# Two of the seven products of FFN layer two through an inner seven-product scheme

## The chip, the cores and the metric

The kernel runs on one core of a Trainium2 chip. A core has five engines with instruction streams of their own: TensorE (PE in the profile, with PEld for its weight loads), VectorE (DVE), ScalarE (ACT), GpSimd (POOL) and SyncE (SP), which here issues the DMA transfers. The engines wait for each other on semaphores. The metric is the device time of one launch in microseconds, lower is better; the kernel before stands at a median of 1946.75 us of three runs (1945.01 to 1947.24).

## The reference

One layer of a hybrid decoder block, for 2048 tokens of width 1024. The front half (a causal pooling mixer and a stick-breaking attention, each normalised, then an output projection) isn't touched. The change is in the feed-forward part behind it:

```python
h = h + jnp.einsum('bse,ed->bsd', mixed, w_out)
hn2 = rmsnorm(h, norm2_g)
up = jnp.einsum('bsd,df->bsf', hn2, w_up)      # 1024 -> 4096
act = jnp.square(jax.nn.relu(up))
h = h + jnp.einsum('bsf,fd->bsd', act, w_down) # 4096 -> 1024
return rmsnorm(h, final_g)
```

All of it is float32.

## The kernel before

A float32 product is made of three matmuls: each operand is split into a hi part (a copy as fp32r, on ACT) and a lo part (the difference, on DVE), and hi x hi, hi x lo and lo x hi are added up in PSUM. `split` does this, L143 on ACT and L144 on DVE.

Activations lie with features on the partitions; a tile is 128 features by T = 512 tokens. The 2048 tokens are four blocks of 512, taken as two pairs q = 0 and q = 1 (`PAIRS`). Both FFN layers multiply with a seven-product scheme (Strassen's, in Winograd's form): the pair gives the rows, features in and out are halved, and P1 to P7 take the place of eight quarter products. Layer one is the function `up`, layer two `down`.

`up` runs over 32 columns, 16 (number m) for each pair q, 7 products of 12 matmuls each (L1016). `post` makes the left operands of layer two from the products: A11, A12, A22 by relu and square on ACT (L949, L950), a21, and on DVE the sums S1 to S4 (L976, L979, L981, L989). `put` (L946) stores each to DRAM, in `sd[q][operand][chunk]`, from a ring of eleven tiles.

`down` goes through the products in the order P1 (A11), P6 (S2), P7 (S3), P4 (A22), P5 (S1), P3 (S4), each in 8 steps kk over both pairs, then P2 (A12) first for q = 0 and then for q = 1. A step loads one weight tile `wr` and a row tile `ar` for each pair (`make`, L1042 and L1073), splits them into `wd` and `ad`, and runs 48 matmuls (L1251; 2 pairs x 4 output chunks x 2 feature chunks x 3). Weight combinations are made on the way with `minus` (L1046) and two of them are kept in DRAM as `td` (L1048). PSUM's eight banks hold the 4 output chunks of both pairs; a sum that several products share goes on in its bank. After a product's last step `evac` copies a bank to SBUF (ACT, L1102) or adds it onto a value there (DVE, L1100). POOL adds the residual h (L1096), which SP loads into one of two `res` tiles (L1095). When both halves of an output block are done, `final` squares them (ACT, L1128) and sums the squares (DVE, L1129). The last two steps of P2 for q = 1 are held back and run in halves of 256 tokens, each with its end right behind it (`last_steps`, L1214).

`make` runs DA = 2 steps ahead in the code. The tile pools limit what can really be ahead: 3 row tiles (`rs`), 4 weight tiles (`rt`), 3 split weights (`t8`), 5 split rows (`s8`), 2 residual tiles (`rsp`). The pools of `down` are laid over memory that `up` has freed, and a tile waits for the last use of what lay there. A scheduler in the framework, with a model of times, sets the order of the instructions on each engine; the SP queue issues in that order, and an issue that has to wait holds all behind it.

The pools of `down` (name and number of tiles):

```python
rlp, tmp2, rs, rt, t8 = spool("rlp", 2), spool("tmp2", 2), spool("rs", 3), spool("rt", 4), spool("t8", DA + 1)
s8, pup, rsp = spool("s8", 2 * DA + 1), spool("pup", 8), spool("rsp", 2)
```

Of the kernel before, what the change touches and what calls it, by code (L numbers as in the profile page):

```python
# [8 lines left out]
F32 = mybir.dt.float32  # L9
# [37 lines left out]
def hymba_block(ctx: ExitStack, tc: tile.TileContext, xT, gains, w_in, pool_w, w_out, w_up, w_down, out):  # L47
# [88 lines left out]
    sd = [[[dram.tile([P, 2, T], F32, name=f"sd{q}_{i}_{c}") for c in range(8)] for i in range(7)] for q in range(2)]  # L136
    td = [[dram.tile([P, 2, T], F32, name=f"td{i}_{c}") for c in range(8)] for i in range(2)]
# [717 lines left out]
    def up(pools, more):  # L855
# [3 lines left out]
        cols = [(q, m) for q in range(2) for m in range(NM)]  # L859
# [14 lines left out]
        def load(q, m):  # L874
            raw[q, m] = (rbb if m % 2 else rba).tile([P, 4, G, P], F32, tag="rb", name="rb")
            nc.sync.dma_start(raw[q, m], w_up[m])
# [63 lines left out]
        def post(q, m, s):  # L940
# [4 lines left out]
            def put(i, t):  # L945
                nc.sync.dma_start(sd[q][i][m // 2][:, m % 2], t)  # L946
# [10 lines left out]
            if s == "P1":  # L957
                copy("p1")
            elif s == "P2":
# [32 lines left out]
        load(0, 0)  # L992
# [9 lines left out]
        load(0, 1)  # L1002
        lefts = [(g, q, s) for g, (q, m, s) in enumerate(slots) if m == 0 and not (q == 0 and s in order[:LB])]
        for g, (q, m, s) in enumerate(slots):
            while lefts and lefts[0][0] <= g + LA:
                make_left(*lefts.pop(0)[1:])
            if q == 0 and 4 <= m < 12 and m % 2 == 0 and s in SUMS:
                sums_second(m // 2 - 2, SUMS.index(s))
# [16 lines left out]
            if g + UA < len(slots):  # L1025
                make_weights(g + UA)
                q2, m2, s2 = slots[g + UA]
                n = q2 * NM + m2 + 2
# [3 lines left out]
    def down(pools):  # L1032
        t8, s8, rs, rt, pup, rsp, rlp, tmp_, psb = pools

        order = (("P1", A11), ("P6", S2), ("P7", S3), ("P4", A22), ("P5", S1), ("P3", S4), ("P2", A12))
        steps = [(n, i, kk, (0, 1)) for n, i in order[:-1] for kk in range(8)]
        steps += [("P2", A12, kk, (q,)) for q in range(2) for kk in range(8)]
        made = {}

# [10 lines left out]

        def make(g):
            n, i, kk, qs_ = steps[g]
            b11, b12, b21, b22 = range(4)
# [4 lines left out]
            elif n == "P6":  # L1058
                w = blk("t1", kk)
                minus(blk(b22, kk), w, 2, kk)  # L1060
# [3 lines left out]
            elif n == "P4":  # L1064
                w = blk("t2", kk)
                minus(blk(b21, kk), w)
            elif n == "P5":
                w = blk("t1", kk)
            else:
                w = blk(b22 if n == "P3" else b21, kk)  # L1070
# [9 lines left out]
            if extra is not None:  # L1080
                minus(blk(b12, kk), extra, 1, kk)
# [4 lines left out]
        CHAIN = {"P1": "p1", "P6": "u2", "P7": "u3", "P4": "c21"}  # L1086
# [11 lines left out]
        def evac(n_, q, n):  # L1098
            b, (j0, j1) = ps[q, n], PAIRS[q]
            add = lambda to, of: nc.vector.tensor_tensor(to[:, n], b, of[:, n], ALU.add)  # L1100
            if n_ in CHAIN:
                nc.scalar.activation(val(CHAIN[n_], q)[:, n], b, AF.Copy)  # L1102
                if n_ in ("P1", "P4"):
                    add_residual(val(CHAIN[n_], q)[:, n], j0 if n_ == "P1" else j1, 0, n)
            elif n_ == "P5":
                add(val("u3", q), val("u3", q))
                add_residual(val("u3", q)[:, n], j1, 1, n)
                add_residual(val("u2", q)[:, n], j0, 1, n)
                if n == 3:
                    final(j1, [val("c21", q)[:, k] for k in range(4)] + [val("u3", q)[:, k] for k in range(4)])  # L1110
            elif n_ == "P3":
                add(val("u2", q), val("u2", q))
                if q == 1:
                    last_half(n, val("u2", q)[:, n])
            else:
                add(val("p1", q), val("p1", q))
                if q == 0 and n == 3:
                    final(j0, [val("p1", q)[:, k] for k in range(4)] + [val("u2", q)[:, k] for k in range(4)])

# [40 lines left out]
        def last_half(n, c):  # L1160
            if n == 0:
                lastv["ss"] = tmp_.tile([P, T], F32, tag="ssl", name="ssl", bufs=1)
                lastv["c"] = {}
            squares(lastv["ss"], c, n == 0)
            lastv["c"][n] = c

        def last_turn():
# [3 lines left out]
            for n in range(4):  # L1171
                t = tmp_.tile([P, T], F32, tag="sq", name="fs")
                nc.scalar.activation(t, lastv["c"][n], AF.Copy, scale=gf[:, 4 + n:5 + n])
                for b in range(TB):
                    nc.tensor.transpose(half[b][:, n * P:(n + 1) * P], t[:, b * P:(b + 1) * P], ident)
            for b in range(TB):
                nc.scalar.activation(res[b // 2][:, b % 2, 1], half[b], AF.Copy)

        def last_steps(operands, j):

            dst = out[j].rearrange("k p t -> (k p t)").rearrange("(b t d) -> t b d", b=TB, d=D)
            ss, c11 = lastv["ss"], val("p1", 1)
# [10 lines left out]
            def finish(th, sq):  # L1193
# [6 lines left out]
                for i in range(2):  # L1200
                    b = 2 * th + i
                    o = lastv["res"][th][:, i]
                    nc.vector.tensor_scalar(o[:, 1], o[:, 1], y[:, i:i + 1], None, op0=ALU.mult)
                    nc.scalar.activation(o[:, 0], half[b], AF.Copy, scale=y[:, i:i + 1])
                    nc.sync.dma_start(dst[:, b], o)

            for th in range(2):
                cols = slice(th * W, (th + 1) * W)
                for n in range(4):
# [8 lines left out]
                    to = c11[:, n, cols]  # L1218
# [6 lines left out]
                    if n == 3:  # L1225
                        nc.vector.tensor_scalar(t, to, gf[:, n:n + 1], None, op0=ALU.mult)
# [202 lines left out]
```

## Time and profile before

| | |
|---|---|
| median of three runs | 1946.75 us (1945.01 to 1947.24) |
| span of the profiled execution, first to last instruction | 1941.4 us |
| the profiled execution's own time | the page gives its span alone |
| front, attention, output projection | 0 to 622 us |
| `up` | 622 to 1308.5 us, a column in 19.04 us |
| `down` | 1309 to 1941 us, a product in 87 us |
| DMA | 426.79 MB, mean 220 GB/s |

How to read it. The page gives the busy time of each engine as a share of the span, then the chain of work that ended last, followed back from the end. A group row reads: line, engine, operation, output tile<-input tiles, shape, count | total busy us, mean ns of one | idle us of the engine just ahead of it and what ended most of this idle time. A row of the timeline starts with start and length in us; `x12` is twelve instructions run together, and the bracket has the idle time ahead of it and its releaser. Rows with SPq are DMA issues. A row of the DMA view has the number of transfers, their size and the median us from issue to landing.

### The profile page before, as it was taken

How to read it: one execution, taken by the hardware profiler on the slowest of the kernel's cores; microseconds unless marked ns; L12 is line 12 of the kernel's file. 1: busy time of each engine (PE TensorE's matmuls, PEld its weight loads, DVE VectorE, ACT ScalarE, POOL GpSimd, SP SyncE). 2: the span in 40 equal slices, each digit the busy share in tenths (PEclk: the TensorE clock that was granted, in tenths of full speed). 3: DMA queues.
4: the chain of work that ended last, by engine and by line, in shares of the span. 5: the costliest groups of instructions: out<-in, count | busy, mean ns of one | idle time of the engine just before them, and what ended most of it. 6: DMA issues, size and time to landing. Idle time of an engine off the chain costs nothing.

```text
span 1941.4 us, 25998 instructions
## 1 busy us (share of the span) xinstructions
PE 1922.7 (99%) x9139; PEld 1605.2 (83%) x9139; DVE 1267.6 (65%) x1882; ACT 956.9 (49%) x1544; POOL 192.0 (10%) x399
## 2 busy tenths in 40 slices
PE   9999999999999999999999999999999999999997
PEld 7888888888888888888888888878888888888887
DVE  6887799668876975777586565665454443446474
ACT  5565566455544555555575555553323233424353
POOL 0211123102111110000000000000110000213010
PEclk9999999999999999999999999999999999999999
DMA  6685686888696954677564544477885554546472
GB/s 216 206 273 180 223 279 208 266 307 285 235 378 233 338 187 155 213 243 247 181 243 159 173 141 158 145 268 288 290 284 196 192 196 151 201 153 208 148 255 89
DMA packets 164845, 426.79 MB, mean 220 GB/s; under 512 B 19680, under 2 KB 25824, under 8 KB 160608
## 3 DMA queue, kind: packets, MB, share of 16 engines
q1 hardware_dynamic: 164560, 424.77, 64.1%
q8 instruction: 74, 1.21, 0.3%
q14 instruction: 67, 0.55, 0.1%
q10 hardware_dynamic: 144, 0.26, 0.0%
HBM read 284.44 MB, written 140.51 MB: 219 GB/s over the span
## 4 chain that ended last, share of the span: by engine, by line
PE 94%; DVE 3%; DMA 2%; ACT 1%; issue 0%; SPq 0%; DVEq 0%; ACTq 0%
PE pb L1251 31%; PE pY L1016 17%; PE pd L173 8%; PE pd L172 8%; PE pd L174 8%; PE pZ L1016 8%; PE pX L1016 4%; PE po L669 2%; PE pta L658 1%; PE pm L199 1%; PE pz L611 1%; PE pz L612 1%; PE pr L225 1%; DMA wr<-in_w_down_dram 1%; PE pb L1214 1%; PE pz L640 0%
## 5 line engine op out<-in xcount | busy, mean ns | idle before, releaser
L1251 PE MATMUL pb<-ad,wd 128*128 128x512 f32 x2640 | 601.6, 390 | 1.3 <-ACT ad L143 0.7
L1251 PEld LDWEIGHTS pb<-ad,wd 128*128 128x128 f32 x2640 | 494.8, 188 | 104.6 <-ACT ad L143 1.3
L1016 PE MATMUL pY<-sa,hw 128*128 128x512 f32 x1536 | 364.3, 390 | 1.2 <-ACT u L955 1.2
L1016 PEld LDWEIGHTS pY<-sa,hw 128*128 128x128 f32 x1536 | 288.1, 188 | 61.8 <-ACT u L955 2.1
L172 PE MATMUL pd<-h,hl 128*128 128x512 f32 x752 | 299.8, 399 | 0.7 <-DVE qkr L418 0.7
L173 PE MATMUL pd<-h,hl 128*128 128x512 f32 x752 | 297.2, 395 | 0.0
L174 PE MATMUL pd<-h,hl 128*128 128x512 f32 x752 | 297.0, 395 | 0.0
L143 ACT ACTIVATE ad<-ar 128x1024 fp32r<-128x1024 f32 x112 | 117.4, 1051 | 139.4 <-PE pb L1251 116.7
L1016 PE MATMUL pZ<-sa,hw 128*128 128x512 f32 x768 | 184.6, 389 | 0.0
L144 DVE TENSOR_TENSOR ad<-ar,ad 128x1024 fp32r<-128x1024 f32 x112 | 144.3, 1293 | 55.6 <-ACT ad L143 55.6
L144 DVE TENSOR_TENSOR wd<-wr,wd 128x1024 fp32r<-128x1024 f32 x64 | 82.2, 1285 | 148.9 <-ACT wd L143 148.4
L143 ACT ACTIVATE wd<-wr 128x1024 fp32r<-128x1024 f32 x64 | 67.8, 1059 | 206.0 <-PE pb L1251 198.3
L1016 PEld LDWEIGHTS pZ<-sa,hw 128*128 128x128 f32 x768 | 144.1, 188 | 29.8
L172 PEld LDWEIGHTS pd<-h,hl 128*128 128x128 f32 x752 | 142.2, 189 | 28.3 <-DVE qkr L418 1.0
L174 PEld LDWEIGHTS pd<-h,hl 128*128 128x128 f32 x752 | 141.9, 189 | 27.9
L173 PEld LDWEIGHTS pd<-h,hl 128*128 128x128 f32 x752 | 142.0, 189 | 26.8
L143 ACT ACTIVATE hl<-raw 128x512 fp32r<-128x512 f32 x168 | 104.2, 630 | 108.2 <-PE pd L174 69.9
L144 DVE TENSOR_TENSOR hl<-raw,hl 128x512 fp32r<-128x512 f32 x168 | 114.6, 687 | 51.3 <-ACT hl L143 50.9
L144 DVE TENSOR_TENSOR hw<-rt,hw 128x512 fp32r<-128x512 f32 x128 | 87.7, 688 | 76.3 <-ACT hw L143 76.1
L1016 PE MATMUL pX<-sa,hw 128*128 128x512 f32 x384 | 93.1, 389 | 0.0
L1046 DVE TENSOR_TENSOR wr<-wr 128x1024 f32<-128x1024 f32 x32 | 39.2, 1224 | 81.0 <-DMA wr<-in_w_down_dram 78.0
L955 ACT ACTIVATE u<-pY 128x512 f32<-128x512 f32 x64 | 38.1, 595 | 103.6 <-PE pY L1016 103.3
(203 smaller groups left out, 2389.7 us busy)
## 6 DMA issues: line engine op xcount, KB each, us to landing
ar<-sd SPq DMA_DIRECT2D x112, 512.0 KB, 4.5
wr<-in_w_down_dram SPq DMA_DIRECT2D x72, 512.0 KB, 3.7
rb<-in_w_up_dram SPq DMA_DIRECT2D x32, 1024.0 KB, 6.1
sd<-a SPq DMA_DIRECT2D x128, 256.0 KB, 3.7
raw<-in_w_in_dram SPq DMA_DIRECT2D x50, 512.0 KB, 4.4
sd<-s SPq DMA_DIRECT2D x96, 256.0 KB, 3.8
raw<-in_w_out_dram SPq DMA_DIRECT2D x32, 512.0 KB, 5.6
sr<-su SPq DMA_DIRECT2D x28, 512.0 KB, 5.5
```

The costliest lines, as they stand in the source:

```text
L143: nc.scalar.activation(hi, src, AF.Copy)
L144: return nc.vector.tensor_tensor(lo, src, hi.bitcast(F32), ALU.subtract)
L172: nc.tensor.matmul(ps, hl[:, 0, c], hi, start=(k == 0), stop=False)
L173: nc.tensor.matmul(ps, hl[:, 0, c], lo, start=False, stop=False)
L174: mm = nc.tensor.matmul(ps, hl[:, 1, c], hi, start=False, stop=(k == n - 1))
L199: marks["pm"] = nc.tensor.matmul(pm[:, c:c + 1], ss[:, c * P:(c + 1) * P], inv[n], start=(i == 0), stop=(i == len(parts) - 1))
L225: mm = nc.tensor.matmul(pr[:, b * P:(b + 1) * P], yr[:, x, b:b + 1].to_broadcast([P, P]), identr, start=(b == 0 and x == 0), stop=(b == TB ...
L669: nc.tensor.matmul(po[:, p * 256 + to:p * 256 + to + hi - lo], vw[:, 2 * p + v], at[:, x, lo:hi], start=(p == 0 and n == 0 and x == 0), sk ...
L955: nc.scalar.activation(k[name], y, AF.Copy)
L1016: nc.tensor.matmul(t, w[:, wx, c], a[:, ax, c % 2], start=first and c == 0 and x == 0, stop=last and c == G - 1 and x == 2, skip_group_che ...
L1046: nc.vector.tensor_tensor(b, a, b, ALU.subtract)
L1251: nc.tensor.matmul(ps[q, n], t[:, wx, c, n * P:(n + 1) * P], left_[q][:, ax, c], start=(n_ in ("P1", "P5", "P2") and kk == 0 and c == 0 an ...
```

## The change

P4 and P2 are no longer run as one product each with 8 steps. Each is a product of a 1024 x 2048 activation (512 tokens of either pair) and a 2048 x 512 weight quarter, and this is split again: the two token pairs give the two row blocks, the features in are halved (columns m and m + 8 of `up`), the 512 outputs are halved. Seven inner products of 4 steps with 12 matmuls take the place of 8 steps with 48. The order of the outer products is now P1, P6, P7, P4 (inner), P5, P2 (inner), and P3 last, for one pair after the other; so the tail works on c12 instead of c11.

What this brings with it:

- `up` takes its columns in the order m, m + 8 (`cols`), so that both halves of an inner row sum are near each other. In the second pair `inner_rows` loads the A22 and A12 tiles of the first pair back (`hr`, L871 of the new listing), and `inner_sums` makes four sums for each and stores them in `sdi` (L880 to L888); A22 and A12 of the first eight columns aren't stored for that pair.
- `inner_weights` makes the four inner weight differences and stores them in `wi`, for P4 during P7 and for P2 during P5 (`prepare`).
- `make_inner` loads and splits an inner step's operands: a weight tile (128 x 1024) holds two steps, a row tile one. `make_ahead` replaces the fixed lead: as many steps as 6 row tiles and 3 weight tiles allow.
- `inner_step` runs the 12 matmuls, and after an inner product's last step DVE adds the bank onto one quarter of the output (c21 or p1) in SBUF.
- P7's evacuation copies its bank twice (u3 and c21). P5's evacuation adds onto u3 and onto u2, the latter formerly in P3. So the squares of the finished blocks fall into P2.
- P6 makes and stores the second `td`, P4 did so before.
- `rs` has 5 tiles and `rt` 6.

```diff
-        cols = [(q, m) for q in range(2) for m in range(NM)]
+        cols = [(q, m + x * (NM // 2)) for q in range(2) for m in range(NM // 2) for x in range(2)]
...
+        def inner_rows(m):
+            for i in (A22, A12):
+                halves[i, 0] = r = srp.tile([P, 2, T], F32, tag="sr", name="hr")
+                for x in range(2):
+                    at = m + x * (NM // 2)
+                    nc.sync.dma_start(r[:, x], sd[0][i][at // 2][:, at % 2])
+
+        def inner_sums(m, i, t):
...
+            a, r = halves.pop((i, 1)), halves.pop((i, 0))
...
+            nc.vector.tensor_tensor(s1, a, t, ALU.add)
+            keep(0, s1)
+            nc.vector.tensor_tensor(s2, s1, r[:, 0], ALU.subtract)
+            keep(1, s2)
+            nc.vector.tensor_tensor(r[:, 0], r[:, 0], a, ALU.subtract)
+            keep(2, r[:, 0])
+            nc.vector.tensor_tensor(r[:, 1], r[:, 1], s2, ALU.subtract)
+            keep(3, r[:, 1])
...
-        order = (("P1", A11), ("P6", S2), ("P7", S3), ("P4", A22), ("P5", S1), ("P3", S4), ("P2", A12))
-        steps = [(n, i, kk, (0, 1)) for n, i in order[:-1] for kk in range(8)]
-        steps += [("P2", A12, kk, (q,)) for q in range(2) for kk in range(8)]
+        SPLIT = {"P4": A22, "P2": A12}
+        order = (("P1", A11), ("P6", S2), ("P7", S3), ("P4", A22), ("P5", S1), ("P2", A12))
+        steps = []
+        for n, i in order:
+            if n in SPLIT:
+                steps += [(n, p, kk, None) for p in ("P1", "P5", "P6", "P3", "P7", "P2", "P4") for kk in range(4)]
+            else:
+                steps += [(n, i, kk, (0, 1)) for kk in range(8)]
+        steps += [("P3", S4, kk, (q,)) for q in range(2) for kk in range(8)]
...
+        def make_inner(n, p, kk):
+            i, kp = SPLIT[n], kk // 2
+            if kk % 2 == 0:
+                if p in wi[i]:
+                    w = rt.tile([P, 4, 256], F32, tag="wr", name="wq")
+                    nc.sync.dma_start(w, wi[i][p][kp])
+                else:
+                    w = quarter(source[n], kp, *{"P1": (0, 0), "P2": (1, 0), "P3": (1, 1)}[p])
+                t = made["inner"] = t8.tile([P, 2, 4, 256], F32R, tag="wd", name="wd", align_bytes=256)
+            r = rs.tile([P, 2, T], F32, tag="ar", name="ar")
...
+            if kk % 2 == 0:
+                split((t[:, 0], t[:, 1]), w)
+            a = s8.tile([P, 2, 2, T], F32R, tag="ad", name="ad", align_bytes=256)
+            split((a[:, 0], a[:, 1]), r)
...
+                if n_ == "P7":
+                    nc.scalar.activation(val("c21", q)[:, n], b, AF.Copy)
+                    add_residual(val("c21", q)[:, n], j1, 0, n)
...
             elif n_ == "P5":
                 add(val("u3", q), val("u3", q))
                 add_residual(val("u3", q)[:, n], j1, 1, n)
+                add(val("u2", q), val("u2", q))
                 add_residual(val("u2", q)[:, n], j0, 1, n)
...
+        def inner_step(n_, p, kk, t, a):
+            tag, q, half = WHERE[p]
+            for i in range(2):
...
+                for c in range(2):
+                    for x, (wx, ax) in enumerate(((0, 0), (0, 1), (1, 0))):
+                        nc.tensor.matmul(b, t[:, wx, 2 * (kk % 2) + c, i * P:(i + 1) * P], a[:, ax, c],
...
+                if kk == 3:
+                    n, name = 2 * half + i, "c21" if n_ == "P4" else "p1"
+                    to = val(name, q)[:, n]
+                    nc.vector.tensor_tensor(to, b, to, ALU.add)
...
+            while ahead[0] < len(steps) and (ahead[1] + lefts(ahead[0]) <= 6 and ahead[2] + stationary(ahead[0]) <= 3):
...
-            rlp, tmp2, rs, rt, t8 = spool("rlp", 2), spool("tmp2", 2), spool("rs", 3), spool("rt", 4), spool("t8", DA + 1)
+            rlp, tmp2, rs, rt, t8 = spool("rlp", 2), spool("tmp2", 2), spool("rs", 5), spool("rt", 6), spool("t8", DA + 1)
```

How it moves the instructions, at the places that the prediction speaks of. The first is the SP queue at the seam of the two layers. A row has the line, the operation, what it writes<-reads, the shape, and in brackets the semaphores that it waits for (DMAHW0 to 7: transfers; the others: engines). Before, loads of `down` (L1042, L1073) stand among the stores of the last columns of `up` (`sd1_..._6` and `_7`, L946):

```order
L946 DMA sd1_5_6_415<-a21_12770 128x512 [waits DMAHW1_49,DVE_49]
L1073 DMA ar_13112<-sd0_0_0_313 128x1024 [waits DMAHW2_49,DVE_49]
L1073 DMA ar_13113<-sd1_0_0_369 128x1024 [waits DMAHW3_49]
L1073 DMA ar_13131<-sd0_0_1_314 128x1024 [waits DMAHW4_49]
L946 DMA sd1_1_6_383<-a12_12796 128x512 [waits DMAHW5_49,Activation_49]
L946 DMA sd1_6_6_423<-s4_12801 128x512 [waits DMAHW6_49,DVE_49]
L946 DMA sd1_0_7_376<-a11_12820 128x512 [waits DMAHW7_49,Activation_49]
L1042 DMA wr_13110<-in_w_down_dram 128x1024 [waits DMAHW0_49]
L1042 DMA wr_13125<-in_w_down_dram 128x1024 [waits DMAHW1_49,PE_49]
L1042 DMA wr_13129<-in_w_down_dram 128x1024 [waits DMAHW2_49]
L1042 DMA wr_13144<-in_w_down_dram 128x1024 [waits DMAHW3_49]
L946 DMA sd1_2_7_392<-a22_12875 128x512 [waits DMAHW4_49,Activation_49]
```

Now all loads of `down` (L1120, L1170) stand behind the last store, and the first waits for three transfers, two of them the stores from `hr_13121`:

```order
L977 DMA sd1_5_7_416<-a21_13267 128x512 [waits DMAHW5_49,DVE_49]
L977 DMA sd1_1_7_384<-a12_13290 128x512 [waits DMAHW6_49,Activation_49]
L880 DMA sdi1_0_3_428<-j1_13295 128x512 [waits DMAHW7_49,DVE_49]
L880 DMA sdi1_1_3_432<-j2_13296 128x512 [waits DMAHW0_49,DVE_49]
L977 DMA sd1_6_7_424<-s4_13305 128x512 [waits DMAHW1_49,DVE_49]
L880 DMA sdi1_2_3_436<-hr_13121 128x512 [waits DMAHW2_49,DVE_49]
L880 DMA sdi1_3_3_440<-hr_13121 128x512 [waits DMAHW3_49,DVE_49]
L1120 DMA wr_13350<-in_w_down_dram 128x1024 [waits DMAHW4_49,DMAHW3_49,DMAHW2_49]
L1170 DMA ar_13352<-sd0_0_0_313 128x1024 [waits DMAHW5_49]
L1170 DMA ar_13353<-sd1_0_0_369 128x1024 [waits DMAHW6_49]
L1120 DMA wr_13365<-in_w_down_dram 128x1024 [waits DMAHW7_49]
```

Moved: the loads of the first steps, from among the stores of the last two columns to behind all of them. On DVE at the same place, the inner sums of the last column pair (L882 to L888) are between the add that makes a12 (L1020) and the first split of `down` (L147):

```order
L1016 TENSOR_TENSOR a21_13267<-a11_13188,a21_13267 128x512 [waits DMAHW6_49]
L1020 TENSOR_TENSOR a12_13290<-pZ_13213,u2_13208 128x512 [waits DMAHW0_49,PE_49]
L882 TENSOR_TENSOR j1_13295<-a12_13165,a12_13290 128x512 [waits DMAHW2_49,Activation_49]
L884 TENSOR_TENSOR j2_13296<-j1_13295,hr_13121 128x512 [waits DVE_49]
L1024 TENSOR_TENSOR s4_13305<-a12_13290,s2_13273 128x512 [waits DMAHW6_49]
L886 TENSOR_TENSOR hr_13121<-hr_13121,a12_13165 128x512 [waits DVE_49]
L888 TENSOR_TENSOR hr_13121<-hr_13121,j2_13296 128x512
L147 TENSOR_TENSOR wd_13356<-wr_13350,wd_13356 128x1024 [waits DMAHW4_49,Activation_49]
L147 TENSOR_TENSOR ad_13359<-ar_13352,ad_13359 128x1024 [waits DMAHW5_49,Activation_49]
L147 TENSOR_TENSOR ad_13362<-ar_13353,ad_13362 128x1024 [waits DMAHW6_49,Activation_49]
```

Added there: j1, j2 and two `hr`; the splits of the first step, formerly between `up`'s last operations, are behind them. The third place is the SP queue where P5 ends, with the residual loads (`res`, L1095, now L1195) among the row loads of the next product. Before (the product is P3, `sd0_6`, `sd1_6`):

```order
L1073 DMA ar_15983<-sd1_6_2_419 128x1024 [waits DMAHW3_49,DVE_49]
L1095 DMA res_15851<-hs0_281 128x512 [waits DMAHW1_49,Pool_49]
L1095 DMA res_15861<-hs1_282 128x512 [waits Pool_49]
L1073 DMA ar_16045<-sd0_6_3_364 128x1024 [waits DMAHW5_49,DVE_49]
L1095 DMA res_15864<-hs0_281 128x512 [waits DMAHW4_49,DMAHW1_49,Pool_49]
L1095 DMA res_15874<-hs1_282 128x512 [waits DMAHW2_49,Pool_49]
L1095 DMA res_15877<-hs0_281 128x512 [waits DMAHW6_49,DMAHW4_49,Pool_49]
L1042 DMA wr_16232<-in_w_down_dram 128x1024 [waits DMAHW7_49,DVE_49]
L1095 DMA res_15911<-hs2_283 128x512 [waits DMAHW5_49,DMAHW0_49,Pool_49]
L1073 DMA ar_16046<-sd1_6_3_420 128x1024 [waits DVE_49]
```

Now (P2's inner products, rows from `sdi1`, `ar_16504` being the third row tile of inner product P6):

```order
L1195 DMA res_16257<-hs0_281 128x512 [waits DMAHW3_49,DMAHW1_49,Pool_49]
L1140 DMA ar_16463<-sdi1_1_0_429 128x1024 [waits DMAHW4_49,DVE_49]
L1195 DMA res_16267<-hs1_282 128x512 [waits DMAHW5_49,DMAHW2_49,Pool_49]
L1195 DMA res_16271<-hs0_281 128x512 [waits DMAHW6_49,DMAHW3_49,Pool_49]
L1195 DMA res_16305<-hs2_283 128x512 [waits DMAHW5_49,Pool_49]
L1195 DMA res_16309<-hs3_284 128x512 [waits DMAHW6_49,DMAHW0_49,Pool_49]
L1135 DMA wq_16624<-wi1_P7_0_461 128x1024 [waits DVE_49]
L1140 DMA ar_16470<-sdi1_1_1_430 128x1024 [waits DVE_49]
L1195 DMA res_16319<-hs2_283 128x512 [waits DMAHW7_49,Pool_49]
L1195 DMA res_16323<-hs3_284 128x512 [waits DMAHW4_49,DMAHW0_49,Pool_49]
L1140 DMA ar_16504<-sdi1_1_2_431 128x1024 [waits DVE_49]
```

Here a `res` load waits for POOL as before, but the row loads between them belong to steps of 12 matmuls instead of 48.

171 lines of the change are left out of this document (121 added, 50 removed).

## The prediction

> **What bounds the kernel now.** I read the page first: busy shares, chain, costliest groups.
>
> ```profile
> span 1941.4 us, 25998 instructions
> PE 1922.7 (99%) x9139; PEld 1605.2 (83%) x9139; DVE 1267.6 (65%) x1882; ACT 956.9 (49%) x1544; POOL 192.0 (10%) x399
> PE 94%; DVE 3%; DMA 2%; ACT 1%; issue 0%; SPq 0%; DVEq 0%; ACTq 0%
> L1251 PE MATMUL pb<-ad,wd 128*128 128x512 f32 x2640 | 601.6, 390 | 1.3 <-ACT ad L143 0.7
> ```
>
> TensorE is busy 99% and carries 94% of the chain that ended last. The second FFN layer (`down`, L1251) idles 1.3 us before 2640 matmuls. So a matmul taken out is worth its whole time, and a wait put in costs its whole time. The table by windows tells what the stages leave free (columns: length, PE, PE loads, DVE, ACT, POOL, clock, DMA share, GB/s): `up`, then P1, P7 and P5 with the start of P3 of `down`, then the tail.
>
> ```profile
> 1100.00:1200.00 100.00, 100.00 (x443) 82.83 (x442) 59.18 (x95) 53.44 (x94) 0.00 (x0) 1.00 0.42 147
> 1312.00:1400.00 88.00, 87.94 (x388) 72.83 (x389) 41.61 (x37) 31.14 (x35) 3.04 (x2) 1.00 0.79 280
> 1490.00:1580.00 90.00, 90.00 (x399) 74.53 (x398) 39.65 (x34) 29.95 (x33) 0.00 (x0) 1.00 0.60 195
> 1660.00:1760.00 100.00, 100.00 (x443) 82.82 (x442) 50.31 (x43) 34.56 (x39) 21.77 (x14) 1.00 0.53 175
> 1910.00:1941.00 31.00, 21.25 (x160) 20.06 (x158) 13.96 (x46) 11.51 (x25) 0.00 (x0) 0.91 0.29 111
> ```
>
> DVE is at 44 to 59%, ACT at 33 to 53%: room on average, so the places where order decides are looked at singly.
>
> **Removed: matmuls.** The chain gives the price of one: 12 in 2.72 us, 24 in 5.44.
>
> ```profile
> 1223.22 5.44 PE pY L1016 x24
> 1228.66 2.72 PE pX L1016 x12
> ```
>
> That is 0.2267 us each. P2 and P4 took 8 steps of 48, 384 each. An inner scheme takes 7 products x 4 steps x 12 = 336. 2 x 48 = 96 fewer: 96 x 0.2267 = **-21.8 us**. An inner product lasts 10.88 us, as one old step did.
>
> **Added at the seam of the two layers: a wait.** Before, the first loads of `down` are issued while `up` computes, and TensorE hardly pauses:
>
> ```profile
> 1278.90 1.27 SPq L1073 DMA_DIRECT2D ar<-sd  x3
> 1283.24 2.96 SPq L1042 DMA_DIRECT2D wr<-in_w_down_dram  x4
> 1305.64 2.88 PE L1016 MATMUL pZ<-sa,hw 128*128 128x512 f32 x12
> 1309.22 2.21 PE L1251 MATMUL pb<-ad,wd 128*128 128x512 f32 x8 [0.70 <-ACT ad L143]
> 1310.19 0.68 DVE L985 TENSOR_TENSOR a<-pZ,u 128x512 f32<-128x512 f32 x1
> 1311.61 0.63 ACT L950 ACTIVATE a<-a 128x512 f32<-128x512 f32 x1
> 1312.06 18.20 PE L1251 MATMUL pb<-ad,wd 128*128 128x512 f32 x79 [0.63 <-DVE ad L144]
> ```
>
> The last `up` matmul ends at 1308.52 (call it E). The pause is 0.70 + 0.63, and the 8 matmuls between took 2.21 instead of 1.81: 1.7 us in all. After the change the first `wr` tile lies over the last `hr` tile of the inner row sums, so its load waits for the last two stores from it, and on SP every first load of `down` stands behind that one. Nothing of `down` can then be prepared before `up` is wholly finished. The new chain, from rows of before: the add L985 starts at E+1.67, and the square of its result ends at 1312.24, E+3.72. Then five DVE operations (four inner sums and s4), 0.60 apart with 0.69 for the last:
>
> ```profile
> 1276.39 0.69 DVE L981 TENSOR_TENSOR a<-a,a 128x512 f32<-128x512 f32 x1
> 1276.99 0.69 DVE L985 TENSOR_TENSOR a<-pZ,u 128x512 f32<-128x512 f32 x1
> ```
>
> 3.1 us, to E+6.8. The store must land, then the load of `wr` and, on the same queue, of `ar`. Landing times, from `up` alone, over the whole page, and of `wr` around the seam, then the rate over 1255 to 1330 us in 40 slices:
>
> ```profile
> sd<-s SPq DMA_DIRECT2D x43, 256.0 KB, 2.2
> sd<-s SPq DMA_DIRECT2D x96, 256.0 KB, 3.8
> DMA to landing us min/median/max: 2.8/5.5/8.4
> GB/s 83 155 181 214 359 356 49 9 140 0 21 156 243 238 286 151 342 421 415 415 253 306 360 413 253 328 335 335 415 383 406 410 412 415 410 208 277 234 269 332
> ```
>
> With 2.2 for the store and 3.0 for a load with an empty queue: E+12.0. `ar`, 512 KB, comes 1.3 us behind it at the 415 GB/s that the busiest slices reach. The hi part of `wd`, meanwhile, and then that of `ad`, 1.05 us each on ACT:
>
> ```profile
> L143 ACT ACTIVATE ad<-ar 128x1024 fp32r<-128x1024 f32 x112 | 117.4, 1051 | 139.4 <-PE pb L1251 116.7
> L144 DVE TENSOR_TENSOR ad<-ar,ad 128x1024 fp32r<-128x1024 f32 x112 | 144.3, 1293 | 55.6 <-ACT ad L143 55.6
> ```
>
> First matmul at E+14.4, net of the old pause **+12.7**. From below: the a12 add at once after E (1.6 less) and minimum landings give +10.6. From above: 3.8 for the store and 5.5 for the load give +16.8.
>
> TensorE then restarts after 14 us idle. The only window here with long idling is the tail: clock 0.91 over 31 us, so at most 2.8 us of clock lost, nothing if all of that fell on idle time. I take **+1.5**. [...]
>
> **Added: splits, and their room.** A split product goes from 24 splits (8 steps of one `wd`, two `ad`) to 42 (7 x (2 + 4)) on ACT and on DVE. One inner product of 10.88 us then asks DVE for 6 x 1.2 + 2 evacuating adds of 0.68 = 8.6, and ACT for 6 x 1.05 = 6.3. It fits alone. In P4 only eight POOL adds (c21) come beside it: I take +0.5 (0 to 2). The 16 subtracts of the inner weights (1.2 us each) lie in P7 and P5, where DVE is busy 40 us of 90: 0; without that cover they would cost 19. The eight subtracts that go from P4 to P6, P7's eight more copies on ACT (0.6 each) and P5's eight adds from P3 (0.68 each) hide the same way, since the product behind them begins in banks that are evacuated first: 0, or 11 us with no cover at all.
>
> A step of the inner schemes loads 512 KB of `ar` and half of a 512 KB `wr` in 2.72 us: 289 GB/s. P1 moved 280 with a DMA share of 0.79 and TensorE hardly idle, so that alone is carried.
>
> P2's inner products begin while POOL adds 16 residuals, formerly under P3 with its 10.9 us steps:
>
> ```profile
> 1735.99 1.23 DVE L144 TENSOR_TENSOR wd<-wr,wd 128x1024 fp32r<-128x1024 f32 x1 [4.21 <-ACT wd L143]
> 1737.90 3.46 POOL L1096 TENSOR_TENSOR u<-u,res 128x512 f32<-128x512 f32 x2 [63.18 <-DVE u L1100]
> 1744.76 1.87 DVE L1100 TENSOR_TENSOR u<-pb,u 128x512 f32<-128x512 f32 x3
> 1747.28 0.63 ACT L1128 ACTIVATE sq<-u 128x512 f32<-128x512 f32 x1 [5.04 <-POOL u L1096]
> 1748.89 2.22 DVE L144 TENSOR_TENSOR wd<-wr,wd 128x1024 fp32r<-128x1024 f32 x1 [0.26 <-ACT wd L143]
> 1751.04 2.31 DVE L144 TENSOR_TENSOR ad<-ar,ad 128x1024 fp32r<-128x1024 f32 x1
> 1773.31 1.71 POOL L1096 TENSOR_TENSOR u<-u,res 128x512 f32<-128x512 f32 x1 [0.84 <-DMA res<-hs]
> L1096 POOL TENSOR_TENSOR u<-u,res x16: 1279/1322/2209, 1673.4 to 1773.3; 128x512 f32<-128x512 f32 x16
> ```
>
> Sixteen adds from 1737.90 to 1775.0 (both token pairs; the first q's loads come early): 2.3 us per add. They start about 9 us ahead of P5's end (the last evacuation ends at 1746.6) and go on 28 us behind it. In those 28 us DVE has 15 splits x 1.2, 5 evacuations x 0.68 and 7 square sums x 0.69: 26 us. Next to a POOL add a split takes 2.22 or 2.31 instead of 1.22; some 12 adds at 0.8 each, since not each meets one, are 10 more. 36 us of work in 28: 8 behind, against a lead of five `ad` tiles in s8, 4 steps of 2.72 or 10.9 us. That just covers it. The `ar` loads of the inner steps also stand on SP behind `res` loads, each of which waits for the POOL add two before it: the third row tile of inner P6 is behind the twelfth `res`, so behind the tenth add, 23 - 9 = 14 us after P5's end. It is used 10 steps in, at 27.2, and must be issued by about 20 (4.5 to land, as the page's `ar` row says, 2.4 to split).
>
> ```profile
> ar<-sd SPq DMA_DIRECT2D x112, 512.0 KB, 4.5
> ```
>
> I take **+2** (0 to 8).
>
> [...]
>
> **Added in `up`.** In the second token pair, 64 sums of 0.60 us on DVE over eight column pairs of 38.08 us: 4.8 each, on top of 59% of 38 (22.5). It fits: 27 of 38. 32 loads and 48 more stores of 256 KB meet a DMA at 147 GB/s. The loads of `hr` stand on SP behind stores that wait for DVE: +0.5 (0 to 2). The tail keeps its shape, with c12 in the place of c11: 0.
>
> **Sum.** -21.8 + 12.7 + 1.5 + 0.5 + 2 + 0.5 = -4.6. The profiled span of 1941.4 becomes 1936.8. The runs' median, 1946.75, lies 5.35 above the span, and I carry this over: **1942.2 us**. With 0.2% (3.9 us) as what a measurement can tell from no change, that is just "faster".
>
> **Rivals.**
> A. The seam costs little: TensorE finds other work, or the last sums go early. Against it: a matmul of `down` needs a tile behind that store on every path, and 10.6 is its floor. With that, 1.0 of clock and no stall: -21.8 + 11.6 = -10.2, 1936.5 us. 0.17.
> B. Slower: the POOL residuals starve P2's inner steps. If both `res` buffers are always waited for, a pair takes a landing of 3.5 and two adds of 2.2, or 3.95 per add:
>
> ```profile
> res<-hs SPq DMA_DIRECT2D x13, 256.0 KB, 3.5
> ...
> L1096 POOL TENSOR_TENSOR u<-u,res 128x512 f32<-128x512 f32 x16 | 24.3, 1522 | 80.7 <-DVE u L1100 63.2 <-DMA res<-hs 15.8 <-DVE ad L144 1.1
> ```
>
> The tenth add then ends 39.5 - 9 = 30.5 us after P5, and the tile named above is 10.5 late; from 2.9 us per add on the queue decides. Stall 10.5 to 15.5 (with DVE 5 further behind) instead of 2: +3.9 to +8.9, so 1951 to 1956, say 1953 us. For it: POOL's waits for `res` in the last row, and the rate, since 256 KB per 2.3 us (114 GB/s) on top of 289 is 403, close to the highest slices. Against: 2.3 per add as seen. 0.25.
> C. The gain is eaten whole: the seam at its upper end (16.8) with the full 2.8 of clock: +0.8, 1947.5 us, no change; the burst of `wr` and `ar` speaks for it (5.5 to land), the empty queue against. 0.12.
> That the matmuls don't fall by 96 is excluded by the order.
>
> **How the numbers follow.** The forecast has 0.46 with its own range 1938 to 1947, a little over half of it faster. Faster: 0.17 + 0.25 = 0.42. Same: 0.21 from the forecast, 0.09 from C, 0.02 from B = 0.32. Slower: 0.23 + 0.03 = 0.26. Leaving out the upper end of B and the lowest of A, the range is 1934 to 1954.
>
> **What would show it.** Right: 2544 matmuls of 128x512 in the main line of `down`; a pause of 13 to 16 us between the last `pZ` and the first `pb`, released by ACT's split, with the `sdi` store and the `wr` load before it in the chain; less than 5 us of TensorE idle in the inner products. Wrong: a pause under 10 or over 20; idle of more than 8 us in P2's inner steps, ended by `ad` splits; columns of `up` in the second pair longer than 19.04 us.

## The result: no change that can be measured

The changed kernel's median is 1946.45 us (12 runs, 1942.82 to 1949.8) against 1944.91 (12 runs, 1941.96 to 1947.25) of the kernel before beside it: ratio 1.0005, 95% interval 0.9997 to 1.0014. The forecast was 4.6 us faster; 1.5 us slower was measured, within 0.2% of no change. The time lies in the range, and the sign of the forecast isn't borne out. The range of 1934 to 1954 us takes in a gain, no change and a loss, so a time inside it says little; the single steps say more.

The page of the changed kernel: its span, busy shares, the chain by engine, and the two groups of matmuls of `down`, outer and inner.

```profile
span 1945.7 us, 26308 instructions
PE 1905.2 (98%) x9043; PEld 1589.0 (82%) x9043; DVE 1384.6 (71%) x2026; ACT 994.7 (51%) x1580; POOL 206.3 (11%) x399
L1391 PE MATMUL pb<-ad,wd 128*128 128x512 f32 x1872 | 429.6, 391 | 16.1 <-ACT ad L146 16.1
L1229 PE MATMUL pb<-ad,wd 128*128 128x512 f32 x672 | 154.3, 390 | 3.4 <-DVE ad L147 3.4
```

1872 + 672 = 2544 matmuls, 96 fewer, as the change says. TensorE is busy 17.5 us less than before, yet the span is 4.3 longer: 16.1 us of idle stand before the outer matmuls and 3.4 before the inner ones. Its own timeline from the last product of `up` on tells where (start, length, operation, count, idle before it and what ended that):

```profile
1308.69 2.88 PE L1051 MATMUL pZ<-sa,hw 128*128 128x512 f32 x12
1327.69 263.85 PE L1391 MATMUL pb<-ad,wd 128*128 128x512 f32 x1152 [16.12 <-ACT ad L146]
1591.38 76.32 PE L1229 MATMUL pb<-ad,wd 128*128 128x512 f32 x336
1667.54 87.20 PE L1391 MATMUL pb<-ad,wd 128*128 128x512 f32 x384
1754.58 17.15 PE L1229 MATMUL pb<-ad,wd 128*128 128x512 f32 x73
1772.31 3.01 PE L1229 MATMUL pb<-ad,wd 128*128 128x512 f32 x12 [0.57 <-DVE ad L147]
1776.24 3.25 PE L1229 MATMUL pb<-ad,wd 128*128 128x512 f32 x13 [0.91 <-DVE ad L147]
1781.39 54.58 PE L1229 MATMUL pb<-ad,wd 128*128 128x512 f32 x238 [1.91 <-DVE ad L147]
1835.81 5.60 PE L1391 MATMUL pb<-ad,wd 128*128 128x512 f32 x24
```

P4's inner scheme runs from 1591.38 to P5's first matmul at 1667.54 (the length of a row reaches a little past the next start): 76.2 us, 336 x 0.2267, without a gap. P2's runs from 1754.58 to 1835.81, 81.2 us, 5.1 above 76.2; 3.4 of these stand as idle, and the rest are smaller delays inside the rows. The pause ahead of `down` is 16.1 us. The chain of waits through it (start, length, what):

```profile
1312.55 0.61 DVE a L1020
...
1313.84 0.64 ACT a L983
...
1317.13 0.61 DVE hr L888
...
1317.90 3.78 DMA sdi<-hr
1321.68 0.02 SPq L1120
...
1322.12 4.44 DMA ar<-sd
...
1326.58 1.07 ACT ad L146
```

With E = 1308.69 + 2.88 = 1311.57: the a12 add at E+1.0, the square ended at E+2.9, the last inner sum at E+6.2; then the store, the load of `wr` (L1120) let go by its landing, the load of `ar` behind that, the split, TensorE at E+16.1. The steps are those that were foreseen. Then the clock, in the table by windows (the column behind POOL's busy time), and the first matmuls in a timeline of the seam alone:

```profile
1312.00:1316.00 4.00, 0.00 (x0) 0.00 (x0) 2.61 (x5) 1.26 (x2) 0.00 (x0) 0.97 0.98 342
1316.00:1320.00 4.00, 0.00 (x0) 0.00 (x0) 1.73 (x3) 0.00 (x0) 0.00 (x0) 0.50 1.05 404
1332.00:1334.00 2.00, 2.00 (x8) 1.58 (x8) 1.95 (x2) 1.78 (x2) 0.00 (x0) 0.78 1.02 408
```

```profile
1327.69 8.63 PE L1391 MATMUL pb<-ad,wd 128*128 128x512 f32 x26 [16.12 <-ACT ad L146]
```

Half clock from 1315.8 (from the 0.97 over 4 us) to 1332.9 (from the 0.78 over 2 us): 26 matmuls take 8.5 us (8.63 with the overlap of the row's end) in place of 26 x 0.2267 = 5.9, 2.6 lost.

### The profile page after: what moved, and what is told of

The parts are those of the page before. It is cut to its first block, busy times and chain, and to the rows that moved or that the text cites. A ratio compares the mean times of both kernels' runs of the same rounds, so it can differ in the third digit from the quotient of the medians.

```text
span 1945.7 us, 26308 instructions
## 1 busy us (share of the span) xinstructions
PE 1905.2 (98%) x9043; PEld 1589.0 (82%) x9043; DVE 1384.6 (71%) x2026; ACT 994.7 (51%) x1580; POOL 206.3 (11%) x399
## 4 chain that ended last, share of the span: by engine, by line
PE 72%; DVE 3%; DMA 1%; issue 1%; ACT 0%; POOL 0%; SPq 0%; DVEq 0%; ACTq 0%
PE pb L1391 21%; PE pY L1051 18%; PE pZ L1051 9%; PE pb L1229 7%; PE pX L1051 4%; PE pd L177 4%; PE pd L175 3%; PE pd L176 3%; PE pb L1334 1%; PE pr L228 1%; DVE ad L147 0%; DVE u L1200 0%; DMA sr<-su 0%; PE pm L202 0%; PE po L672 0%
## 5 line engine op out<-in xcount | busy, mean ns | idle before, releaser
L1391 PE MATMUL pb<-ad,wd 128*128 128x512 f32 x1872 | 429.6, 391 | 16.1 <-ACT ad L146 16.1
L1391 PEld LDWEIGHTS pb<-ad,wd 128*128 128x128 f32 x1872 | 352.6, 189 | 89.6 <-ACT ad L146 16.5
L147 DVE TENSOR_TENSOR ad<-ar,ad 128x1024 fp32r<-128x1024 f32 x136 | 175.6, 1300 | 50.5 <-ACT ad L146 50.2
L146 ACT ACTIVATE ad<-ar 128x1024 fp32r<-128x1024 f32 x136 | 142.5, 1051 | 115.3 <-PE pb L1391 69.1
L1229 PE MATMUL pb<-ad,wd 128*128 128x512 f32 x672 | 154.3, 390 | 3.4 <-DVE ad L147 3.4
L1229 PEld LDWEIGHTS pb<-ad,wd 128*128 128x128 f32 x672 | 125.6, 188 | 31.8 <-DVE ad L147 5.9
L147 DVE TENSOR_TENSOR hl<-raw,hl 128x512 fp32r<-128x512 f32 x168 | 114.6, 687 | 51.1 <-ACT hl L146 48.1
L147 DVE TENSOR_TENSOR hw<-rt,hw 128x512 fp32r<-128x512 f32 x128 | 87.6, 687 | 72.8 <-ACT hw L146 72.7
L146 ACT ACTIVATE wd<-wr 128x1024 fp32r<-128x1024 f32 x48 | 50.9, 1060 | 147.4 <-PE pb L1391 111.6
L147 DVE TENSOR_TENSOR wd<-wr,wd 128x1024 fp32r<-128x1024 f32 x48 | 58.8, 1224 | 67.6 <-ACT wd L146 67.3
```

The lines of the kernel that those rows point to most:

```text
L146: nc.scalar.activation(hi, src, AF.Copy)
L147: return nc.vector.tensor_tensor(lo, src, hi.bitcast(F32), ALU.subtract)
L1229: nc.tensor.matmul(b, t[:, wx, 2 * (kk % 2) + c, i * P:(i + 1) * P], a[:, ax, c], start=p in ("P1", "P5", "P2") and kk == 0 and c == 0 and ...
L1391: nc.tensor.matmul(ps[q, n], t[:, wx, c, n * P:(n + 1) * P], left_[q][:, ax, c], start=(n_ in ("P1", "P5", "P3") and kk == 0 and c == 0 an ...
```

## The experiments

Every kernel is the changed one with the edit shown. Beside the first four the kernel before had a median of 1945.61 us (31 runs), beside the last three 1945.48 (9 runs).

**1. The inner row sums in the ring of small tiles**, so that no load of `down` waits for them.

```diff
-                halves[i, 0] = r = srp.tile([P, 2, T], F32, tag="sr", name="hr")
+                halves[i, 0] = r = [avp.tile([P, T], F32, tag="av", name="hr") for _ in range(2)]
...
-            nc.vector.tensor_tensor(r[:, 0], r[:, 0], a, ALU.subtract)
+            nc.vector.tensor_tensor(r[0], r[0], a, ALU.subtract)
...
```

> The loaded rows of the inner sums (hr) go into the ring of small activation tiles instead of the pool under down's first loads; the sums and all else stay. Theory (the first wr load waits for the last stores from hr, because its tile lies over it): the loads of down go out among the last columns of up again, the pause before the first pb falls from 16.1 us to about 4 or 5 (the a12 add and its relu stand ahead of the first ad split), the clock loss behind it from 2.6 us to 0 to 1.5: 11 to 13 us less than the changed kernel, about 1934 us. Rival (the wait is for the sums' data itself, or for TensorE's last products): the pause stays above 14 us and the time at 1946. A second rival: the ring is too small for four more tiles, up's columns of the second pair get longer than 19.04 us, and the gain is lost there.

Measured: 1941.46 us (12 runs), ratio 0.9979 (0.9968 to 0.9989). The pause is 9.8 us, not 4 to 5. TensorE's timeline of this kernel, then DVE's (same columns):

```profile
1310.02 3.02 PE L1051 MATMUL pZ<-sa,hw 128*128 128x512 f32 x12 [1.20 <-DVE a L1004]
1322.85 22.46 PE L1391 MATMUL pb<-ad,wd 128*128 128x512 f32 x92 [9.81 <-ACT ad L146]
```

```profile
1302.28 1.23 DVE L147 TENSOR_TENSOR wd<-wr,wd 128x1024 fp32r<-128x1024 f32 x1 [1.65 <-ACT wd L146]
1319.71 0.69 DVE L1014 TENSOR_TENSOR s<-s,a 128x512 f32<-128x512 f32 x1 [4.30 <-DMA sd<-a]
```

The split of the first `wd` stands at 1302.28, ahead of E: the weight loads had really waited for the `hr` tile alone, and the theory holds there. What is left is a new wait: a ring of eleven small tiles that now also holds `hr` runs out (experiment 7 gives it two more, and this wait is gone). A sum of `up` waits 4.3 us for the store of an earlier tile to land, and the last relu and the `ad` split stand behind it on ACT. Those splits, now ahead of E on DVE, also hold up the last column (1.20 us, ended by DVE's L1004). So the gain is 5 us and not 11 to 13. The profiled execution, at 1945.85 us, is 4.4 above the median: its P2 takes 84.8 us (1748.62 to 1833.41), and the 191 matmuls behind its last wait take 46.29 us in place of 191 x 0.2267 = 43.30, as about 6 us at half clock would make (an estimate).

**2. One residual moved**: the residual of output half u2 is added at P6's evacuation, with P6's matmuls behind it, instead of at P5's.

```diff
                 elif n_ == "P1":
                     add_residual(val("p1", q)[:, n], j0, 0, n)
+                else:
+                    add_residual(val("u2", q)[:, n], j0, 1, n)
...
                 add(val("u2", q), val("u2", q))
-                add_residual(val("u2", q)[:, n], j0, 1, n)
```

> The residual of u2 is added when P6 is evacuated instead of P5: 8 of the 16 POOL adds, their 8 res loads leave P2's inner products. Theory (DVE, slowed beside POOL's adds, feeds P2's inner steps late): P2's 28 steps, 81.2 us against 76.2 of matmul time, go to 77 to 78, idle before ad splits from 3.4 us to under 1; 3 to 4 us less than the changed kernel, about 1943. Rival (the short steps themselves are fed too slowly, by queue or DMA rate): the 81.2 stays, time 1946. The pause between up and down stays at 16 us in both.

Measured: 1939.6 us (8 runs), ratio 0.9971 (0.9958 to 0.9984). TensorE's timeline:

```profile
1754.86 76.63 PE L1230 MATMUL pb<-ad,wd 128*128 128x512 f32 x336
```

P2's inner steps take 76.5 us without a gap, 4.8 less than with the change alone; the pause at the seam stays at 15.9. The stall hung on those eight adds, four for each pair, and their loads; experiments 5 and 6 take the two apart. The medians moved by 6.8 us, which the intervals allow to be 4.8, and the spans of the two profiled executions differ by 4.5 (1945.7 and 1941.2).

**3. The row sums into fresh tiles**, so that `hr` is only read: the load of `wr` then waits for the reads of DVE and not for the stores to land.

```diff
-            nc.vector.tensor_tensor(r[:, 0], r[:, 0], a, ALU.subtract)
-            keep(2, r[:, 0])
-            nc.vector.tensor_tensor(r[:, 1], r[:, 1], s2, ALU.subtract)
-            keep(3, r[:, 1])
+            s3, s4 = (avp.tile([P, T], F32, tag="av", name=n) for n in ("j3", "j4"))
+            nc.vector.tensor_tensor(s3, r[:, 0], a, ALU.subtract)
+            keep(2, s3)
+            nc.vector.tensor_tensor(s4, r[:, 1], s2, ALU.subtract)
+            keep(3, s4)
```

> The last two inner sums are written into fresh small tiles instead of onto hr, so hr is free when DVE has read it, and not when its store has landed. Theory (the chain add, relu and square, five DVE operations, store, load, split): the store's 3.8 us leave the chain, the pause falls from 16.1 to 12 to 13 us, 3 to 4 us less, about 1943; the clock loss stays. Rival (the pause is set by something else, such as the last product or the splits): 16 us and 1946.

Measured: 1945.1 us (11 runs), ratio 1.0 (0.9991 to 1.0009). The pause is 15.0. Its chain of waits:

```profile
1311.23 0.61 DVE j L889
...
1312.35 0.42 SPq L1121
...
1313.79 6.50 DMA ar<-sd
...
1320.31 1.07 ACT ad L146
```

The store is out of the chain, as the edit wants: with E = 1306.4 here the load of `ar` goes out at E+7.4 and not at E+10.6. But it lands after 6.50 us instead of 4.44: 2.1 of the 3.2 us are given back. I take it that it now shares the DMA with the last stores: 345 GB/s are moved from 1312 to 1316 here, and 33 from 1321 to 1323 around the issue of the changed kernel's load. The expected gain failed on that.

**4. TensorE kept busy through the pause**, with 140 products of the identity into a bank that nothing reads.

```diff
+        warm = bank(WB)
+        for _ in range(WN):
+            nc.tensor.matmul(warm[:, :P], identr, identr, start=True, stop=True, skip_group_check=True)
```

> 140 matmuls of 128x128 of a constant, whose result nothing reads, stand on TensorE between the last product of up and the first of down. They are estimated at 0.1 us each (the pr rows: 8 in 0.89), 14 us, so they end before the first data of down. Theory (the 26 matmuls behind the pause take 8.6 us instead of 5.9 because the clock falls in the idle time): granted clock near 1.0 behind the pause, the first 26 in 5.9 us, time 2 to 2.7 us less than the changed kernel, about 1944. Rival (these matmuls are slow because the lo splits of the first step come late): 8.6 us again, no gain.

Measured: 1947.38 us (12 runs), ratio 1.0014 (1.0002 to 1.0026). TensorE's timeline, then the clock in half microseconds:

```profile
1307.67 15.75 PE L1375 MATMUL pb<-identr 128*128 128x128 f32 x140
1326.34 0.80 PE L1395 MATMUL pb<-ad,wd 128*128 128x512 f32 x1 [2.92 <-ACT ad L147]
1327.60 8.76 PE L1395 MATMUL pb<-ad,wd 128*128 128x512 f32 x30 [0.47 <-DVE ad L148]
```

```profile
1324.00:1324.50 0.50, 0.00 (x0) 0.00 (x0) 0.00 (x0) 0.00 (x0) 0.00 (x0) 0.83 0.94 344
1331.00:1331.50 0.50, 0.50 (x3) 0.36 (x3) 0.44 (x2) 0.42 (x1) 0.00 (x0) 0.84 1.02 410
```

The products ended at 1323.4, but the load of `ar` took 6.97 us to land, against 4.44 without them (why was not settled), and 2.9 us were left. The clock fell at 1324.3 already, 0.9 us behind the products, and stayed at half to 1331.2. So nothing follows for what a warm clock is worth here.

**5. P5's residuals without their loads**: the 16 POOL adds stay, but take a tile that is in SBUF already.

```diff
-                add_residual(val("u2", q)[:, n], j0, 1, n)
...
+                for name in ("u3", "u2"):
+                    add(val(name, q), val(name, q))
+                    to = val(name, q)[:, n]
+                    nc.gpsimd.tensor_tensor(to, to, rlast[:, 0], ALU.add)
```

> The 16 residual adds behind P5 stay on POOL but add a tile that is in SBUF already; the 16 res loads are left out (so the residual of two output halves isn't added). Theory (DVE's two-input operations run at about half speed beside POOL's adds): the adds now follow each other without waits for res, DVE is slowed as often as before, and P2's 28 steps still take 79 to 82 us, with idle before ad splits of 2 to 5 us. Rival (the res loads, on SP ahead of the row loads, and their share of the DMA rate starve the steps): 76.5 us, no idle.

One run: 1943.75 us. TensorE's timeline of P2, then DVE's:

```profile
1750.76 16.93 PE L1229 MATMUL pb<-ad,wd 128*128 128x512 f32 x74
1769.74 2.81 PE L1229 MATMUL pb<-ad,wd 128*128 128x512 f32 x11 [2.04 <-DVE ad L147]
1773.67 3.28 PE L1229 MATMUL pb<-ad,wd 128*128 128x512 f32 x13 [1.12 <-DVE ad L147]
1777.13 54.25 PE L1229 MATMUL pb<-ad,wd 128*128 128x512 f32 x238 [0.18 <-DVE ad L147]
1831.21 5.60 PE L1391 MATMUL pb<-ad,wd 128*128 128x512 f32 x24
```

```profile
1763.46 2.31 DVE L147 TENSOR_TENSOR wd<-wq,wd 128x1024 fp32r<-128x1024 f32 x1
1765.69 1.78 DVE L1249 TENSOR_TENSOR ss<-ss,sq 128x512 f32<-128x512 f32 x1
1774.73 1.21 DVE L147 TENSOR_TENSOR wd<-wq,wd 128x1024 fp32r<-128x1024 f32 x1
```

P2 takes 80.5 us, 4.2 above 76.2, with no residual load on SP at all: adds alone make such a stall. By the difference 0.9 of the changed kernel's 5.1 would be the queue's, but the adds stand closer together here, so this isn't a bound. From 1757 to 1773, while POOL adds, a split takes 2.3 us and a sum of squares 1.78; behind the last add 1.21 and 0.68.

**6. The same adds made short**: P5's residuals are loaded, but only one column of 512 is added.

```diff
-            nc.gpsimd.tensor_tensor(t, t, r, ALU.add)
+            nc.gpsimd.tensor_tensor(t[:, :w], t[:, :w], r[:, :w], ALU.add)
...
```

> The 16 res loads behind P5 stay, on the same queue and with the same waits, but POOL adds one column of 512 of each (the rest of the residual is left out). Theory (POOL's adds slow DVE): P2's 28 steps take 76.2 to 77 us, DVE's splits there 1.2 us each, none above 1.5. Rival (res loads starve the steps): 79 us or more.

One run: 1947.15 us. No split in P2 takes more than 1.23 us, where beside full adds it took 2.31 in experiment 5, so the length there is the adds' doing. But P2 takes 83.6 us (1751.49 to 1835.12), as the rival has it: the stall is another one. SP's timeline (the length covers its waits), and ACT's:

```profile
1755.90 13.82 SPq L1195 DMA_DIRECT2D res<-hs  x5
...
1772.92 0.90 SPq L1140 DMA_DIRECT2D ar<-sdi  x2
```

```profile
1778.75 1.06 ACT L146 ACTIVATE ad<-ar 128x1024 fp32r<-128x1024 f32 x1 [13.14 <-DMA ar<-sdi]
```

In this kernel's order five residual loads stand in a row on SP, each behind an earlier add, and the next row tile is issued 17 us later: the queue of rival B. One add holds it up most (the view of the tile `res`, with min/median/max in ns):

```profile
L1196 POOL TENSOR_TENSOR u<-u,res x16: 184/190/7362, 1743.8 to 1780.8; 128x1 f32<-128x1 f32 x16
```

A one-column add that takes 0.19 us elsewhere lasts 7.36, from 1757.47 to 1764.83. In all of that time DVE runs splits and sums of squares, with both inputs in SBUF, and the add ends 0.13 us after DVE has turned to an operation that reads PSUM (L1236, at 1764.70). So both ways were measured: in experiment 5 a split takes 2.31 us for 1.21 beside an add, here an add takes 7.36 for 0.19 beside splits and sums. I take it that the queue is long here in part because of DVE. Of P2's 7.4 us, 4.2 are idle, and most of the rest is in the matmuls behind them: 12 from 1781.12 on take 5.38 us in place of 2.72, as at half clock (an estimate).

The expected 76 to 77 us fell. It doesn't contradict experiment 5: two ways lead from the residuals to a starved P2. In the changed kernel DVE is busy without a break from 1750 to 1798 and its splits end all three waits, so there the first, DVE's, decides; here DVE stands idle for 11 us, waiting for the row tile.

**7. Both places mended**: edits 1 and 2 together, a ring of thirteen small tiles, paid for by three row tiles in `srp`.

```diff
-SR = 4
+SR = 3
...
-            ... spool("avp", 11)
+            ... spool("avp", 13)
```

> The hr tiles in the small ring, which has 13 tiles now instead of 11 (the pool that hr left has three instead of four), and the residual of u2 added at P6. Theory (in the run with 11 tiles the pause was 9.8 us because s2 waited 4.3 us for a free tile, and the last columns lost 2 us the same way; P2's stall is POOL's adds): pause 4 to 6 us, clock loss under 1.5, P2 in 76.5 us: 10 to 11 for the seam, 1 to 2 for the clock and 5 for P2 less than the changed kernel, 1929 to 1932 us, about 0.99 of the kernel before. Rival (what holds s2 is the landing of stores behind the burst of down's loads, whatever the ring): pause 9 to 10 and 1936.

Measured: 1929.46 us (5 runs, 1927.93 to 1930.55), ratio 0.9917 (0.9904 to 0.9931): 16 us faster than the kernel before, and faster than the changed one too. TensorE's timeline:

```profile
1314.65 30.62 PE L1392 MATMUL pb<-ad,wd 128*128 128x512 f32 x124 [5.83 <-ACT ad L146]
1741.32 76.47 PE L1230 MATMUL pb<-ad,wd 128*128 128x512 f32 x336
```

The pause is 5.8 us and P2 76.3. The clock loss is 2.4 (half clock from the first matmul to 1319.37), not under 1.5 as expected. Against experiment 2, which differs in the place of the sums' rows and the pools of `up`, the median is 10.1 us lower and the pause 10.1 us shorter. That agrees with a price of one microsecond for one of this pause; the intervals leave room for 3 to 4 us either way.

## Why the prediction missed, step by step

| term | predicted us | measured us |
|---|---|---|
| 96 matmuls | -21.8 | -21.8 |
| pause at the seam, net of 1.7 before | +12.7 | +14.4 |
| clock after it | +1.5 | +2.6 |
| P4 inner | +0.5 | 0 |
| P2 inner | +2 | +5.1 |
| `up` | +0.5 | not found |
| behind P2 | 0 | +0.9 |
| sum | -4.6 | +1.2 |

The sum, +1.2, is what the two profiles show from E on (632.9 us to the end before, 634.1 after); the 0.9 is what is left of that, and the one new wait seen in it is 0.54 us for POOL's `yr`. The medians moved by +1.5. The span grew by 4.3: 3.05 more lie ahead of E (1308.52 before, 1311.57 after), and they aren't there in every profile of kernels whose `up` is the changed one's: E is 1307.8 in experiment 4 and 1308.2 in experiment 5. Of these 1.7 are the clock in one place, below; the columns of the second pair take 19.04 us as before.

**Removed matmuls**: right, in number and in price.

**The seam**: the mechanism was right, link by link, and the size was off by 1.7. The step that failed is "with 2.2 for the store and 3.0 for a load with an empty queue". DVE was done 0.6 earlier than reckoned (E+6.2 for 6.8), but the store took 3.78 to land, 3.9 with its issue, and the two loads 4.9 for 4.3. The store went into a burst: the windows show 342 and 404 GB/s, from the other last stores of `up`. The loads did find an empty queue, as assumed (33 GB/s from 1321 to 1323); `wr` took 3.54 us all the same, and `ar` landed 1.3 behind it. So the store is the term that was mis-sized most, 3.9 for 2.2. The prediction had 3.8 in its quoted rows and took the quiet stretch's 2.2 for a place where all stores of the last column come together.

**The clock**: taken as +1.5 from the tail's bound of 2.8; 2.6 were measured. That bound came from the one stretch of before with long idling; here 5.2 us of matmuls passed at half clock (1327.69 to 1332.86, more in the last section), and half of that is the 2.6.

**P2's inner steps**: mis-sized, 5.1 for 2, within the bounds of 0 to 8. The step that failed is "that just covers it". The mechanism held: in the changed kernel a split next to an add takes 2.3 us, DVE is busy without a break, and three waits are ended by its splits. Rows of DVE there:

```profile
1763.73 2.32 DVE L147 TENSOR_TENSOR ad<-ar,ad 128x1024 fp32r<-128x1024 f32 x1
1765.97 1.77 DVE L1249 TENSOR_TENSOR ss<-ss,sq 128x512 f32<-128x512 f32 x1
1779.04 4.52 DVE L147 TENSOR_TENSOR ad<-ar,ad 128x1024 fp32r<-128x1024 f32 x2
```

Beside an add a split takes 1.1 us longer there (2.32 for 1.21) and a sum of squares as much (1.77 for 0.68), not the 0.8 for each add that was set for "not each meets one". Experiments 5 and 6 agree for the splits, 2.31 beside adds of full length and at most 1.23 beside adds of one column. The size of the stall also varies: in experiments 4, 3 and 1, which leave P2 as it is, the profiles show 4.7, 7.3 and 8.6 us above 76.2, the last with 3.0 of it in slow matmuls.

**The rivals**: A fell, since the pause was 16.1. B's second half (DVE behind) decided, without the queue; the queue as a cause was seen in experiment 6 only, and there the longest add, 7.36 us, stood beside DVE's splits and sums. C came nearest in time, 1947.5, and nearly in kind: seam and clock cost 17.0 us of its 19.6, and P2 the rest. The forecast had the seam and P2 in the lower half of their bounds; four errors of one sign, 6.8 us, less two of the other, 1.0, make up the 5.8 between -4.6 and +1.2.

## What to carry to other kernels

Where a change reuses memory across a seam of two stages, look for the first load behind it on each queue: one tile that it waits for held back everything queued after it here, 16.1 us of pause, and the 21.8 us saved elsewhere on TensorE were gone. Price transfers at such a seam by rows from a burst, not from a quiet stretch (3.78 us for the store here, priced at 2.2). Where fast steps take the place of slow ones, work of other engines that was hidden (here POOL's residual adds) has to be moved under a slow stage as well (P2 went from 81.2 to 76.5 us in experiment 2); that move, with the sums' rows in a slightly larger ring of small tiles, turned a change worth nothing into 0.8%.

## What the runs showed of the hardware

At the places measured here the clock stayed at half for 3.41 us or 2, 3 or 5 times that, and in `up` it fell behind waits of 1.8 to 2.1 us. At the seam of the changed kernel it falls at 1315.80 and returns at 1332.86, worked out from these two half microseconds:

```profile
1315.50:1316.00 0.50, 0.00 (x0) 0.00 (x0) 0.50 (x2) 0.00 (x0) 0.00 (x0) 0.80 1.07 414
1332.50:1333.00 0.50, 0.50 (x3) 0.39 (x2) 0.45 (x2) 0.28 (x2) 0.00 (x0) 0.64 1.00 401
```

That is 17.06 us; in experiment 1 it is 10.24 (1315.43 to 1325.67), in 4 it is 6.83 (1324.33 to 1331.16): 5, 3 and 2 times 3.41. So the restart was paid from the first matmul to the return of the clock: 5.2 us at half clock in the changed kernel, 2.8 in experiment 1 (1322.85 to 1325.67). A wait also cost time behind it. In the changed kernel's `up` TensorE waits 1.77 us, and 12 matmuls take 4.5 us behind it in place of 2.7 to 2.9:

```profile
1004.03 4.54 PE L1051 MATMUL pY<-sa,hw 128*128 128x512 f32 x12 [1.77 <-ACT u L988]
```

The clock around it, by windows:

```profile
1005.00:1005.50 0.50, 0.50 (x3) 0.35 (x3) 0.50 (x2) 0.50 (x2) 0.00 (x0) 0.68 0.36 143
1008.50:1009.00 0.50, 0.50 (x4) 0.42 (x3) 0.00 (x0) 0.50 (x2) 0.00 (x0) 0.91 0.25 98
```

The clock falls at 1005.18, while TensorE is busy, and returns at 1008.59, 3.41 later. The falls at 1005.18 and 1315.80 are 310.62 us apart, 91 times 3.413. Experiments 2 and 5 fall in both places as well, 310.61 apart each (1005.76 and 1316.37, 1001.16 and 1311.77). From these I take, as an estimate, ticks 3.413 us apart, and call the stretch between two of them a window. The same wait in six other profiles, with the windows carried back from each one's own fall at the seam; the granted clock from 1000 to 1012 us was 0.86 in the three with a fall and 1.00 in the others:

| profile | wait us | of it in one window | window busy | clock fell |
|---|---|---|---|---|
| experiment 5 | 2.06 | 2.06 | 40% | yes |
| experiment 2 | 1.89 | 1.89 | 45% | yes |
| the change | 1.77 | 1.77 | 48% | yes |
| experiment 6 | 1.60 | 1.60 | 53% | no |
| experiment 4 | 1.59 | 1.59 | 53% | no |
| experiment 1 | 2.07 | 1.55 | 55% | no |
| experiment 7 | 1.68 | 0.95 | 72% | no |

By this estimate experiment 1's wait of 2.07 us lay across a tick, and the 12 matmuls behind it took 3.02 us; the change's 1.77 lay in one window, and they took 4.54, with 1.7 us of clock in it: profiles differ by this without any difference in the work. The busy share, as the trace has it, gives no sharp line: in experiment 1's P2 the 47 matmuls behind a window busy for an estimated 46% (1769.41 to 1772.83) ran without such a loss (11.02 us), and in experiment 4 the clock fell behind one busy for 73%, mostly with the 128x128 products (1320.92 to 1324.33). At half clock, windows that were busy for 52% (the change, 1326.04 to 1329.45) and 66% (experiment 2, 1326.61 to 1330.03) ended without a return of the clock, and one busy for 83% ended with it (experiment 1, 1322.26 to 1325.67). The wait stands where `up` goes over to its second token pair: the ACT copy that ends it is behind a split before which ACT waits for the load of a row tile (`sr`, 5.50 us in the changed kernel, 4.26 before). Why it makes TensorE wait 1.6 to 2.1 us in seven profiles, not at all in experiment 3 and 0.53 in the one of before was left open; the change may have a part of 1 us in it.
